# A two-layer decoder trunk: six of the seventeen chunks that TensorE transposes are turned by VectorE's block transposes and gathers from two queues

## The chip, the cores and the metric

The kernel runs on one core of one Trainium2 chip. A core has five engines that are programmed apart: TensorE (PE in the profile, with its weight loads as PEld), VectorE (DVE), ScalarE (ACT), GpSimd (POOL) and SyncE (SP). Each takes its instructions strictly in order and waits on semaphores that others raise. Data lies in the on-chip memory SBUF; TensorE writes its sums to a second memory, PSUM. DMA transfers are issued here by SP and POOL. An issue stands in the order of its engine's queue like any other instruction.

The metric is the device time of one execution in microseconds (us), lower is better. The kernel before takes 2478.81 us, the median of three runs (2478.05 to 2479.55).

## The reference

A trunk of two layers over 256 positions of width 2048, float32. Each layer is

```
h = RMSNorm(x)
q, k, v, uv, gate_logits = split(h @ w_in)                 # 2048 -> 7680
branch_a = sliding_window_attention(q, k, v) @ w_attn_branch
branch_b = chunked_sgu(gelu(uv)) @ w_sgu_branch
merged = gates_a * branch_a + gates_b * branch_b
x = x + merged @ w_out
h2 = RMSNorm(x)
x = x + (silu(h2 @ w_gate) * (h2 @ w_up)) @ w_down         # 2048 -> 5632 -> 2048
```

Nearly all of the work is products of a 256-row activation with large weights, and every weight is read once from the DRAM.

## The kernel before

**Products.** A weight is cut into column chunks of 512 (CW). A piece of 256 rows by 512 columns (a "half", 512 KB) is loaded by SP (L198, `raw`), and split into two parts whose sum keeps nearly the whole float32: ScalarE copies it to `whi` (L221), VectorE subtracts to get `wlo` (L222). The activation has to lie transposed, with the contraction along the 128 partitions, and is split the same way into `uh` and `ul`. TensorE then adds three products for each block, `uh*whi`, `uh*wlo` and `ul*whi` (L310, L311), each a matmul of 128x128 with 128x512. A half feeds 12 matmuls. Pairs of chunks (gate and up, or two columns of w_out or w_down) go by a scheme with seven products in place of eight for one quarter of the contraction. Its sums are formed by VectorE (L209 for the weights, L335 for the results), and its six first pieces, of six matmuls each, are laid between the last halves of the product before.

**Steps.** `Stream` loads seven pieces ahead (W_LOAD) and splits four ahead (W_SPLIT); there are five `raw` buffers and four of `whi` and of `wlo`. After every 12 matmuls (two of the six-matmul pieces, or one half) `tick()` runs. `after(n, fn)` puts work n ticks later, and everything beside the matmuls (norms, gelu, attention, transposes) is laid out with it. TensorE keeps the order in which the code is written; the other engines' order is made by a scheduler with a timeline of its own, so the diff alone doesn't tell where an instruction lands.

**Transposed chunks.** `transposed()` makes `uh` and `ul` of one chunk of 512 columns (a "unit"). It has two ways. With `on_pe`, TensorE transposes the chunk in eight matmuls of 128x128 against the identity (L421, tile `pt` in PSUM), and ScalarE and VectorE make `uh` and `ul` from PSUM in the same step. Without it, `turn()` lets VectorE transpose 32x32 blocks of each half of the chunk into `box` (L379, two instructions, one tick apart); 16 DMAs of 32 KB then carry the blocks to their places in `tt` (L384), issued by POOL for units of the residual and hidden chunks and by SP for queries, keys, attention outputs and the gating unit's outputs; six and seven steps after the DMAs (plus `late`), ScalarE and VectorE split `tt` into `uh` and `ul`. There is one `box` buffer.

**Which chunks go by TensorE.** Seventeen: the four of the input; the last chunk of `merged` in each layer; the last chunk of x before the feed-forward part in each layer (`nxt.unit(3)`, L859); three of the four chunks of x before the second layer; and the last hidden chunk of each of the three rounds of the feed-forward part in each layer (L949, L950). The rounds hold four, four and three chunks of 512. Each is a last chunk of an activation, produced only a few steps before the next product wants it. The product that follows a round, or follows the residual, begins with chunk 1, so the last of four chunks is wanted last.

Of the kernel before, what the change touches and what calls it, by code (L numbers as in the profile page):

```python
# [30 lines left out]
B = 32  # L31
# [26 lines left out]
def hybrid_trunk(ctx: ExitStack, tc: tile.TileContext, x, mix_norm, w_in, q_norm, k_norm, sinks,  # L58
# [313 lines left out]
    def turn(dst, src, queue):  # L372


        box = turned.tile([P, 4, 4, NT, B], F32, tag="box", name=nm("box"))
        iv = src.rearrange("p t (k j c) -> p t k j c", j=4, c=B)

        def blocks(t):
            nc.vector.transpose(box[:, :, :, t, :].rearrange("p j k r -> p k j r"), iv[:, t])  # L379

        def gather():
            for j in range(4):
                for i in range(4):
                    queue.dma_start(dst[j * B:(j + 1) * B, i], box[i * B:(i + 1) * B, j])  # L384

        blocks(0)
        after(1, lambda: (blocks(1), gather()))

    def transposed(units, c, src, cols=None, on_pe=False, wino=None, again=False, queue=None, late=0):

# [33 lines left out]
            return  # L424

        tt = slot([P, 4, 4, NT, B], name="tt")
        turn(tt, src, queue or nc.gpsimd)
# [51 lines left out]
    class Norm:  # L479
# [10 lines left out]
                nc.scalar.activation(junk, xs[:, t, c * CW:(c + 1) * CW], AF.Square,  # L490
                                     accum_out=self.ss[t][:, c:c + 1])

        def unit(self, c, on_pe=False, again=False):
            transposed(self.units, c, xs[:, :, c * CW:(c + 1) * CW], cols=self.cols[:, 4 * c:4 * c + 4],
                       on_pe=on_pe, again=again,
                       wino=None if c != WINO or on_pe else WINO_FIRST if again else WINO_IN if self.soon else
                       WINO_NORM)

# [346 lines left out]
    def residual(key, nxt=None, scale=1.0, store=False):  # L845

        def chunk(j, sums):
# [22 lines left out]
    for l in range(DEPTH):  # L870
# [65 lines left out]
        def hidden(hT, c):  # L936
# [8 lines left out]
            def on_up(up):  # L945
                for t in range(NT):
                    nc.vector.scalar_tensor_tensor(out=hid[:, t, :], in0=up[t], scalar=norm.rr[t], in1=hid[:, t, :],
                                                   op0=ALU.mult, op1=ALU.mult)
# [54 lines left out]
```

## Time and profile before

| | |
|---|---|
| median of three runs | 2478.81 us |
| profiled execution | 2476.85 us, of which the span 2475.1 us |
| TensorE (PE) busy | 2462.7 us, 99% |
| VectorE (DVE) busy | 1929.7 us, 78% |
| ScalarE (ACT) busy | 1430.2 us, 58% |
| GpSimd (POOL) busy | 282.8 us, 11% |
| DMA | 502.54 MB, 203 GB/s, queue of SP 59.8% of 16 engines |
| granted TensorE clock | 1.0 |

The span runs from the first to the last instruction of the program; the time of an execution has 1.75 us around it. A row of a timeline gives the start in us, the duration, engine, line, operation, tiles (written<-read), and in brackets how long the engine had been idle before it and what ended that. Matmuls overlap, so the distance between two starts is what one costs TensorE, not its duration. In a group's row, the numbers after the count are min/median/max in ns. A row of waits gives the engine and line that waited, whom for, us in total, times, and the longest.

### The profile page before, as it was taken

To read this page: it belongs to the slowest core of one execution; us is meant where nothing else is said; L and a number is where in the kernel's file an instruction comes from. 1 tells how busy PE (TensorE), PEld (TensorE's weight loads), DVE (VectorE), ACT (ScalarE), POOL (GpSimd) and SP (SyncE) were. 2 spreads that over 40 slices of the span, in tenths; PEclk is the share of its full clock that TensorE was granted. 3 is DMA by queue.
4 is the path that set the end of the run, shared out by engine and by line. 5 is a ranking of instruction groups with operands and counts; after the bars stand their busy time and mean duration, and the time that the engine had idled before them with its cause. 6 is when DMAs were issued, how large, how long until landed. Compare 5 with 4: busy or idle time off the path is not lost.

```text
span 2475.1 us, 31205 instructions
## 1 busy us (share of the span) xinstructions
PE 2462.7 (99%) x11088; PEld 2027.7 (82%) x11088; DVE 1929.7 (78%) x2261; ACT 1430.2 (58%) x1794; POOL 282.8 (11%) x527
## 2 busy tenths in 40 slices
PE   9999999999999999999999999999999999999999
PEld 7888888888888888888888888888888888888887
DVE  6798676887877787778887986768878777877786
ACT  5566544575655565556655665446655555655564
POOL 3100002221110111001101000121212001110110
PEclk9999999999999999999999999999999999999999
DMA  8655656576656666575747446666657566656654
GB/s 295 205 176 166 213 198 218 181 240 194 214 195 205 211 191 226 174 226 186 229 152 266 153 160 219 214 203 196 227 186 233 183 218 195 215 196 201 216 191 150
DMA packets 275661, 502.54 MB, mean 203 GB/s; under 512 B 26224, under 2 KB 36048, under 8 KB 275504
## 3 DMA queue, kind: packets, MB, share of 16 engines
q1 hardware_dynamic: 259472, 484.25, 59.8%
q0 software_dynamic: 15712, 16.01, 2.2%
q8 instruction: 87, 1.43, 0.2%
q14 instruction: 70, 0.57, 0.1%
q10 hardware_dynamic: 320, 0.27, 0.0%
HBM read 475.27 MB, written 2.10 MB: 193 GB/s over the span
## 4 chain that ended last, share of the span: by engine, by line
PE 93%; DVE 4%; issue 1%; DMA 1%; ACT 1%; SPq 0%; POOL 0%; DVEq 0%; ACTq 0%
PE acc L310 60%; PE acc L311 30%; DVE wlo L222 2%; DMA raw<-in_w_in_dram 1%; PE po L758 1%; DVE raw L209 1%; PE pt L421 1%; ACT whi L221 0%; PE psc L719 0%; PE ppt L748 0%; PE psg L836 0%; DVE ul L412 0%; DVE kept L335 0%; SPq L384 0%; DVE box L379 0%
## 5 line engine op out<-in xcount | busy, mean ns | idle before, releaser
L222 DVE TENSOR_TENSOR wlo<-raw,whi 128x1024 fp32r<-128x1024 f32 (+1 forms) x1039 | 1265.7, 1220 | 494.6 <-ACT whi L221 481.4
L221 ACT ACTIVATE whi<-raw 128x1024 fp32r<-128x1024 f32 (+1 forms) x1039 | 1098.0, 1058 | 924.6 <-PE acc L311 750.7
L310 PE MATMUL acc<-whi,uh 128*128 128x512 f32 x3114 | 1217.2, 391 | 0.4 <-ACT whi L221 0.2
L310 PE MATMUL acc<-wlo,uh 128*128 128x512 f32 x3114 | 1212.7, 389 | 1.5 <-DVE wlo L222 1.4
L311 PE MATMUL acc<-whi,ul 128*128 128x512 f32 x3114 | 1212.3, 389 | 0.0
L310 PEld LDWEIGHTS acc<-wlo,uh 128*128 128x128 f32 x3114 | 584.7, 188 | 124.5 <-DVE wlo L222 3.9
L311 PEld LDWEIGHTS acc<-whi,ul 128*128 128x128 f32 x3114 | 584.4, 188 | 122.6 <-DVE ul L412 0.2
L310 PEld LDWEIGHTS acc<-whi,uh 128*128 128x128 f32 x3114 | 584.6, 188 | 121.3 <-ACT uh L407 0.8
L384 POOL DMA_DIRECT2D tt<-box x480 | 236.0, 498 | 1714.5 <-DVE box L379 949.9
L209 DVE TENSOR_TENSOR raw<-raw,raw 128x1024 f32<-128x1024 f32 x188 | 229.3, 1220 | 1.3
L310 PE MATMUL acc<-wlo,sh 128*128 128x512 f32 x376 | 151.3, 402 | 3.3 <-DVE kept L335 3.3
L310 PE MATMUL acc<-whi,sh 128*128 128x512 f32 x376 | 147.2, 392 | 0.0
L311 PE MATMUL acc<-whi,sl 128*128 128x512 f32 x376 | 146.7, 390 | 0.0
L310 PEld LDWEIGHTS acc<-wlo,sh 128*128 128x128 f32 x376 | 70.5, 188 | 27.6 <-DVE kept L335 14.5
L311 PEld LDWEIGHTS acc<-whi,sl 128*128 128x128 f32 x376 | 70.6, 188 | 15.2
L310 PEld LDWEIGHTS acc<-whi,sh 128*128 128x128 f32 x376 | 70.7, 188 | 13.2
L335 DVE TENSOR_TENSOR kept<-acc,kept 128x512 f32<-128x512 f32 x94 | 64.1, 682 | 0.0
L338 ACT ACTIVATE acc<-kept 128x512 f32<-128x512 f32 x94 | 54.0, 587 | 8.5 <-DVE kept L335 8.3
L853 DVE SCALAR_TENSOR_TENSOR xs<-acc,xs 128x512 f32<-128x512 f32 (+1 forms) x66 | 41.2, 666 | 7.8 <-PE acc L311 7.8
L942 ACT ACTIVATE hid<-acc,rhalf 128x512 f32<-128x512 f32 x44 | 30.4, 690 | 21.0 <-PE acc L311 21.0
L332 ACT ACTIVATE kept<-acc 128x512 f32<-128x512 f32 x47 | 28.1, 597 | 15.0 <-PE acc L311 15.0
L943 DVE SCALAR_TENSOR_TENSOR hid<-hid,acc 128x512 f32<-128x512 f32 x44 | 29.6, 684 | 8.3 <-ACT hid L942 8.3
(135 smaller groups left out, 878.0 us busy)
## 6 DMA issues: line engine op xcount, KB each, us to landing
raw<-in_w_in_dram SPq DMA_DIRECT2D x239, 512.0 KB, 4.6
raw<-in_w_up_dram SPq DMA_DIRECT2D x176, 512.0 KB, 4.7
raw<-in_w_gate_dram SPq DMA_DIRECT2D x176, 512.0 KB, 4.6
raw<-in_w_down_dram SPq DMA_DIRECT2D x176, 512.0 KB, 4.6
raw<-in_w_out_dram SPq DMA_DIRECT2D x64, 512.0 KB, 4.8
raw<-in_w_attn_branch_dram SPq DMA_DIRECT2D x32, 512.0 KB, 5.5
raw<-in_w_sgu_branch_dram SPq DMA_DIRECT2D x32, 512.0 KB, 4.3
tt<-box POOLq DMA_DIRECT2D x480, 32.0 KB, 4.1
```

The lines of the kernel that those rows point to most:

```text
L209: self.last = nc.vector.tensor_tensor(out=self.raws[d], in0=self.raws[x], in1=self.raws[y], op=ALU.subtract)
L221: nc.scalar.activation(hi[:, i, :], raw[:, i, :], AF.Copy)
L222: self.last = nc.vector.tensor_tensor(out=lo[:, i, :], in0=raw[:, i, :], in1=hi[:, i, :].bitcast(F32), op=ALU.subtract)
L310: nc.tensor.matmul(ps, a, part[:, kk, :], start=first and kk + n == 0, stop=False, skip_group_check=True)
L311: nc.tensor.matmul(ps, b, hi[:, kk, :], start=False, stop=kk == 1, skip_group_check=True)
L332: nc.scalar.activation(p.kept[:, 1, :], a[0], AF.Copy)
L335: nc.vector.tensor_tensor(out=p.kept[:, int(tag == "P7"), :], in0=a[1], in1=p.kept[:, 1, :], op=ALU.add)
L338: nc.scalar.activation(ps, p.kept[:, t, :], AF.Copy)
L384: queue.dma_start(dst[j * B:(j + 1) * B, i], box[i * B:(i + 1) * B, j])
L853: nc.vector.scalar_tensor_tensor(out=xs[:, t, sl], in0=sums[t][:, i * w:(i + 1) * w], scalar=scale, in1=xs[:, t, sl], op0=ALU.mult, op1=AL ...
L942: nc.scalar.activation(th, g[t], AF.Tanh, scale=norm.rh[t])
L943: nc.vector.scalar_tensor_tensor(out=th, in0=th, scalar=1.0, in1=g[t], op0=ALU.add, op1=ALU.mult)
```

## The change

Six of the seventeen chunks go the other way: the last chunk of x before the feed-forward part (both layers) and the last hidden chunk of the two rounds with four chunks (both layers). Eleven still go by TensorE. For the six, `transposed()` is called one tick after the chunk's result in place of three, VectorE transposes the blocks, the 16 DMAs are shared by SP and POOL, eight each, and the split comes four and five steps after the start of `turn` (`late=-2`), two sooner than for other turned chunks.

```diff
         def gather():
             for j in range(4):
                 for i in range(4):
-                    queue.dma_start(dst[j * B:(j + 1) * B, i], box[i * B:(i + 1) * B, j])
+                    q = queue if queue is not None else (nc.sync, nc.gpsimd)[i % 2]
+                    q.dma_start(dst[j * B:(j + 1) * B, i], box[i * B:(i + 1) * B, j])
...
-        def unit(self, c, on_pe=False, again=False):
+        def unit(self, c, on_pe=False, again=False, queue=nc.gpsimd, late=0):
             transposed(self.units, c, xs[:, :, c * CW:(c + 1) * CW], cols=self.cols[:, 4 * c:4 * c + 4],
-                       on_pe=on_pe, again=again,
+                       on_pe=on_pe, again=again, queue=queue, late=late,
...
-                after(3 if j == NCH - 1 and not nxt.soon else 2, lambda: nxt.unit(j, j == NCH - 1 or j > 0 and nxt.soon))
+                last = j == NCH - 1 and not nxt.soon
+                after(1 if last else 2, lambda: nxt.unit(j, j > 0 and nxt.soon, queue=None if last else nc.gpsimd,
+                                                         late=-2 if last else 0))
...
-                pe = c == len(hT) - 1
-                after(3 if pe else 2, lambda: transposed(hT, c, hid, on_pe=pe, wino=WINO_HID if c == WINO else None))
+                pe, soon = c == len(hT) - 1 == 2, c == 3
+                after(3 if pe else 1 if soon else 2,
+                      lambda: transposed(hT, c, hid, on_pe=pe, wino=WINO_HID if c == WINO else None,
+                                         queue=None if soon else nc.gpsimd, late=-2 if soon else 0))
```

On TensorE the change takes out two rows of four transposes at each of the six places and moves nothing else. On the other engines the order around one hidden chunk (the first round of layer 0) and around one chunk of x (layer 0) shows what is moved. Line numbers of the changed kernel are one higher from L385 on.

VectorE at the hidden chunk, before (L947 makes the chunk, L404 splits it from `pt`):

```order
L947 TENSOR_SCALAR hid_6003<-acc_6057,rr_965_5005,hid_6003 128x512
L947 TENSOR_SCALAR hid_6003<-acc_6058,rr_969_5014,hid_6003 128x512
L222 TENSOR_TENSOR wlo_6348<-raw_6171,whi_6347 128x1024
L222 TENSOR_TENSOR wlo_6360<-raw_6312,whi_6359 128x1024
L222 TENSOR_TENSOR wlo_6398<-raw_6325,whi_6397 128x1024
L404 TENSOR_TENSOR ul_6380<-pt_6381,uh_6379 128x512
L404 TENSOR_TENSOR ul_6380<-pt_6388,uh_6379 128x512
L222 TENSOR_TENSOR wlo_6418<-raw_6345,whi_6417 128x1024
```

and after (L379 are the block transposes, L405 splits the chunk from `tt`):

```order
L379 STREAM_TRANSPOSE box_6358<-hid_6013 128x4x4x32
L222 TENSOR_TENSOR wlo_6363<-raw_6181,whi_6362 128x1024
L379 STREAM_TRANSPOSE box_6358<-hid_6013 128x4x4x32
L222 TENSOR_TENSOR wlo_6392<-raw_6322,whi_6391 128x1024
L222 TENSOR_TENSOR wlo_6414<-raw_6335,whi_6413 128x1024
L222 TENSOR_TENSOR wlo_6434<-raw_6360,whi_6433 128x1024
L222 TENSOR_TENSOR wlo_6446<-raw_6389,whi_6445 128x1024
L222 TENSOR_TENSOR wlo_6464<-raw_6411,whi_6463 128x1024
L222 TENSOR_TENSOR wlo_6484<-raw_6429,whi_6483 128x1024
L209 TENSOR_TENSOR raw_6429<-raw_6431,raw_6429 128x1024
L222 TENSOR_TENSOR wlo_6503<-raw_6443,whi_6502 128x1024
L405 TENSOR_TENSOR ul_6356<-tt_6357,uh_6355 128x512 x2
```

Two block transposes are added around the first subtraction behind the chunk, and the split moves five subtractions later. ScalarE's two copies to `uh` move the same way, behind five more `whi`.

SP at the hidden chunk, after (before, the same loads stand there without the row of `tt`):

```order
L198 DMA raw_6411<-in_w_down_dram 128x2x512
L198 DMA raw_6520<-in_w_down_dram 128x2x512
L385 DMA tt_6357<-box_6358 32x256 x8
L198 DMA raw_6443<-in_w_down_dram 128x2x512
L198 DMA raw_6481<-in_w_down_dram 128x2x512
```

Eight DMAs of the gather stand between two loads of weights; POOL has the other eight, with nothing else near them at this place.

ScalarE at the chunk of x, before (L407 scales and copies to `uh`; `tt_4727` is chunk 2, `pt` is chunk 3):

```order
L407 ACTIVATE uh_4725<-tt_4727,vcols 128x256 x4
L407 ACTIVATE uh_4952<-pt_4954,vcols 128x256 x2
L407 ACTIVATE uh_4952<-pt_4965,vcols 128x256 x2
L221 ACTIVATE whi_5020<-raw_4918 128x1024
L221 ACTIVATE whi_5032<-raw_4930 128x1024
```

and after:

```order
L408 ACTIVATE uh_4725<-tt_4727,vcols 128x256 x4
L221 ACTIVATE whi_5018<-raw_4923 128x1024
L221 ACTIVATE whi_5030<-raw_4952 128x1024
L221 ACTIVATE whi_5052<-raw_4978 128x1024
L221 ACTIVATE whi_5076<-raw_5014 128x1024
L221 ACTIVATE whi_5095<-raw_5028 128x1024
L221 ACTIVATE whi_5115<-raw_5014 128x1024
L408 ACTIVATE uh_4917<-tt_4919,vcols 128x256 x4
```

The four copies of chunk 3 move behind six weight copies. On VectorE the eight subtractions of chunk 3 (L413) move behind the same six pieces' `wlo`, and the two block transposes stand together two subtractions behind the chunk's sums (L854). On POOL the eight DMAs stand ahead of the two `rstd` of the norm. From the place of the removed transposes to the first matmul that reads the unit, TensorE's order has 102 matmuls of L310 and L311 at each of the six places.

More of the change, by code (lines that the diff above doesn't have):

```diff
@@ L383, in gather, with transposed @@
                 for i in range(4):
-                    queue.dma_start(dst[j * B:(j + 1) * B, i], box[i * B:(i + 1) * B, j])
+                    q = queue if queue is not None else (nc.sync, nc.gpsimd)[i % 2]
+                    q.dma_start(dst[j * B:(j + 1) * B, i], box[i * B:(i + 1) * B, j])
         blocks(0)
         after(1, lambda: (blocks(1), gather()))
-    def transposed(units, c, src, cols=None, on_pe=False, wino=None, again=False, queue=None, late=0):
+    def transposed(units, c, src, cols=None, on_pe=False, wino=None, again=False, queue=nc.gpsimd, late=0):
         uh, ul = units[c] if again else (slot([P, 4, S], F32R, "uh"), slot([P, 4, S], F32R, "ul"))
@@ L426, in transposed @@
         tt = slot([P, 4, 4, NT, B], name="tt")
-        turn(tt, src, queue or nc.gpsimd)
+        turn(tt, src, queue)
         def blocks_of(k0):
```

## The prediction

> **What bounds the kernel now.** I read the page first: the busy shares, the clock, the chain of work that ended last.
>
> ```profile
> span 2475.1 us, 31205 instructions
> PE 2462.7 (99%) x11088; PEld 2027.7 (82%) x11088; DVE 1929.7 (78%) x2261; ACT 1430.2 (58%) x1794; POOL 282.8 (11%) x527
> PEclk9999999999999999999999999999999999999999
> PE 93%; DVE 4%; issue 1%; DMA 1%; ACT 1%; SPq 0%; POOL 0%; DVEq 0%; ACTq 0%
> ```
>
> TensorE is the bound in every slice, at full clock, and 93% of the chain is its matmuls. Whatever leaves its queue shortens the program, unless it then waits. So the next view is its waits, taken from 45 us on to leave out the start (the last row, ScalarE's, is of the whole span):
>
> ```profile
> PEld acc L310 <- DVE kept L335: 15.0, 42, 1.3
> PEld acc L310 <- DVE wlo L222: 0.4, 1, 0.4
> PE acc L310 <- DVE kept L335: 3.3, 4, 0.9
> ...
> ACT uh L403 <- DMA tt<-box: 9.3, 5, 3.4
> ```
>
> In 2430 us TensorE waited once, for 0.4 us, for a split weight. The rows of `kept` belong to the sums of the seven-product scheme, which the change leaves alone. Loads, splits and the turns that SP carries already are hidden.
>
> **What a transposed chunk costs TensorE.** The timeline of TensorE at a hidden chunk and at a chunk of x:
>
> ```profile
> 720.41 0.40 PE L311 MATMUL acc<-whi,ul 128*128 128x512 f32 x1
> 720.64 1.04 PE L421 MATMUL pt<-ident,hid 128*128 128x128 f32 x8
> 721.44 0.48 PE L310 MATMUL acc<-whi,uh 128*128 128x512 f32 x1
> ...
> 550.45 0.39 PE L311 MATMUL acc<-whi,ul 128*128 128x512 f32 x1
> 550.68 1.04 PE L421 MATMUL pt<-ident,xs 128*128 128x128 f32 x8
> 551.47 0.48 PE L310 MATMUL acc<-whi,uh 128*128 128x512 f32 x1
> 551.78 0.40 PE L310 MATMUL acc<-wlo,uh 128*128 128x512 f32 x1
> ...
> 2205.99 1.03 PE L421 MATMUL pt<-ident,hid 128*128 128x128 f32 x8
> 2206.78 0.48 PE L310 MATMUL acc<-whi,uh 128*128 128x512 f32 x1
> ...
> L421 PE MATMUL pt<-ident,hid x48: 270/272/273, 720.6 to 2421.9; 128*128 128x128 f32 x48
> ```
>
> Matmuls start 0.23 us apart (550.45 to 550.68). Eight transposes hold the next matmul back from 720.64 to 721.44, 0.80 us, and the one after it comes 0.31 us later (551.47 to 551.78) in place of 0.23, another 0.08. No wait stands in these rows. One chunk therefore costs 0.88 us, and the last of the six places reads the same (2205.99 to 2206.78). Six chunks: 6 x 0.88 = 5.3 us, all of it on the engine that sets the end.
>
> The Trainium skill ("TensorE: Matmul & The Clock Gate", Part 4: PE-mode transpose) gives about 275 ns for one such transpose in a kernel's context; by that as a price, 48 of them would be worth an estimated 13.2 us. The rows agree with it as a duration (272 ns) and not as a price, since eight of them take 0.80 us.
>
> **What is added, engine by engine.**
>
> ```profile
> L379 DVE STREAM_TRANSPOSE box<-hid x32: 700/705/708, 593.6 to 2376.2; 128x512 f32<-128x512 f32 x32
> L404 DVE TENSOR_TENSOR ul<-tt,uh x44: 647/684/692, 210.4 to 2396.8; 128x512 fp32r<-128x512 f32 x44
> L404 DVE TENSOR_TENSOR ul<-pt,uh x16: 677/681/684, 466.3 to 2424.2; 128x512 fp32r<-128x512 f32 x16
> ...
> 716.56 1.40 DVE L947 SCALAR_TENSOR_TENSOR hid<-acc,rr,hid 128x512 f32<-128x512 f32 x2
> 717.90 2.58 DVE L222 TENSOR_TENSOR wlo<-raw,whi 128x1024 fp32r<-128x1024 f32 x2
> 721.98 1.23 DVE L222 TENSOR_TENSOR wlo<-raw,whi 128x1024 fp32r<-128x1024 f32 x1 [1.50 <-ACT whi L221]
> ```
>
> VectorE gets two block transposes for each chunk, 2 x 0.705 = 1.41 us. The split costs the same from `tt` as from `pt` (684 and 681 ns). At the hidden chunk the two stand before 721.98, where VectorE was idle for 1.50 us, so they fit and cost nothing. At the chunk of x the eight subtractions of chunk 3 (2.16 us in the rows below) leave the crowded stretch as the 1.41 us enter it, so VectorE is earlier there.
>
> ```profile
> 550.11 1.23 DVE L222 TENSOR_TENSOR wlo<-raw,whi 128x1024 fp32r<-128x1024 f32 x1 [0.95 <-ACT whi L221]
> 555.50 2.16 DVE L412 SCALAR_TENSOR_TENSOR ul<-pt,vcols,uh 128x128 fp32r<-128x128 f32 x8
> 567.87 1.23 DVE L222 TENSOR_TENSOR wlo<-raw,whi 128x1024 fp32r<-128x1024 f32 x1 [1.54 <-ACT whi L221]
> 570.59 2.59 DVE L222 TENSOR_TENSOR wlo<-raw,whi 128x1024 fp32r<-128x1024 f32 x2 [1.49 <-ACT whi L221]
> ...
> 551.89 1.69 ACT L407 ACTIVATE uh<-tt,vcols 128x256 fp32r<-128x256 f32 x4
> 566.77 1.06 ACT L221 ACTIVATE whi<-raw 128x1024 fp32r<-128x1024 f32 x1 [1.71 <-PE acc L311]
> ...
> 734.01 1.06 ACT L221 ACTIVATE whi<-raw 128x1024 fp32r<-128x1024 f32 x1 [1.66 <-PE acc L311]
> ```
>
> **Is the unit there in time?** By the order, 102 matmuls lie between the removed transposes and the first reader. At 0.23 us each that is 23.5 us: 744.1 at the hidden chunk, 574.2 at the chunk of x. At the hidden chunk ScalarE's copies stand behind the `whi` of 734.01, so from 735.1 on, and `ul` follows by about 737.6: over 6 us to spare. At the chunk of x the copies stand behind the `whi` of 566.77, from 567.8 on; VectorE's eight subtractions follow the `wlo` of 567.87, from 569.1 for 2.2 us, to 571.3: 2.9 us to spare. These starts are set by TensorE's own progress ("<-PE acc L311"), so all move earlier together.
>
> The copies must also find `tt` landed.
>
> ```profile
> L384 POOL DMA_DIRECT2D tt<-box x480: 496/498/570, 45.5 to 2386.8; - x160
> L384 SPq DMA_DIRECT2D tt<-box x192: 507/588/1082, 88.0 to 1550.3; - x192
> DMA to landing us min/median/max: 1.6/3.8/8.4
> ...
> 1540.87 10.01 SPq L384 DMA_DIRECT2D tt<-box  x16
> 1550.98 2.06 SPq L198 DMA_DIRECT2D raw<-in_w_attn_branch_dram  x4
> ...
> 719.15 1.73 SPq L198 DMA_DIRECT2D raw<-in_w_down_dram  x2
> raw<-in_w_down_dram SPq DMA_DIRECT2D x176, 512.0 KB, 4.6
> ```
>
> `box` is full at about 717.9 + 0.7 + 1.2 + 0.7 = 720.5 at the hidden chunk and, behind the `wlo` that ends at 551.3, at 552.7 at the chunk of x. POOL issues eight in 8 x 0.5 = 4 us. With the longest landing seen, 8.4 us, `tt` is there by 732.9 and 565.1, each over 2 us ahead of the copies. POOL's two `rstd` at the chunk of x come some 2 us later; `hid` needs them only at the first gate, far behind.
>
> On SP the eight issues stand ahead of a load. The nearest row is a turn of sixteen: 10.01 us, no load in between, then the loads catch up. Twelve such turns (192 issues) are in the trace, and the row of waits above bounds what they cost TensorE at 0.4 us in all. Half a turn, 5 us, is bounded by 0 below and by 0.4/12 = 0.03 us for each above; I take 0. Above that lies only a wait that adds up with another, which the rivals price. A gain beyond 5.3 has no source I can see: none of the six places had TensorE waiting.
>
> **The sum.** -5.3 us on TensorE, 0 from VectorE, ScalarE, SP and POOL. From the profiled execution, 2476.85 - 5.3 = 2471.5. That execution lies 1.96 us below the median of the runs, 2478.81, and the forecast is made for the median: 2473.5 us, -0.21%. A difference of 0.2%, 5.0 us, is about what a measurement of this kernel can tell from no change, so the forecast lies just beyond that bound.
>
> **Rivals.**
>
> *Given back in part.* One or two of the places return what they save, as a wait for `ul` or for a sum of the seven-product scheme that VectorE's displaced work delays. For it: the two places at x have only 2.9 us of slack, and behind them VectorE works without a break from 570.59 to 573.2. Against: VectorE's idle time of 1.5 us ahead of most `wlo`. Two places lost: -3.5 us, 2475.3.
>
> *POOL's DMAs starve (slower).* If each of POOL's eight issues had to wait for a subtraction of `wlo` (1.23 us, row 567.87), they would take 8 x 1.7 = 13.8 us; with 8.4 us to land, `tt` is there at 552.7 + 22.2 = 574.9 at x and 742.7 at the hidden chunk. ScalarE would stand at the copies for 7 us. `ul` would come at about 578.5 at x (a copy, a `wlo` and 2.2 us later) against 574.2, and at 745.3 at the hidden chunk (two copies and two splits) against 744.1: 2 x 4.3 + 4 x 1.2 = 13.4 us, net +8.1, 2486.9. It turns to a loss when the eight issues take over 12 us, since from 9.5 us on each more costs the two places at x as much: 2 x (12.2 - 9.5) = 5.4. The rows speak against it: 480 issues between 496 and 570 ns while VectorE is 78% busy. The Trainium skill ("SBUF — State Buffer", SBUF: two separate sides) describes just this, POOL unable to write descriptors while VectorE holds a shared port in a two-port mode; no row here shows it.
>
> *SP blocks the weights (slower).* Behind the eight gathers the load that was issued at about 720.5 (the second in the row of 719.15) comes 5 us later. It is first read by the `whi` of 734.01, and loads land in 4.6 us, so its slack is 734.0 - 720.9 - 4.6 = 8.5 us. That `whi` starts when TensorE is done with the fourth piece ahead, so three pieces of 12 x 0.23 us lie between, 8.3, less 1.06 and 1.23 for the split: 6 more. SP could stand for 14.5 us; each us beyond costs TensorE one at each place, and from 15.4 on (5.3 / 6 = 0.9) the change loses. At 16.5 it would be 6 x 2 - 5.3 = +6.7, 2485.5. The row of 10.01 us speaks against it.
>
> *Transposes dearer than their spacing.* 48 x 0.273 = 13.1 us gained, 2465.7, if they did not overlap; the rows show that they do.
>
> **How the numbers follow.** Forecast 0.74, given back in part 0.12, POOL 0.05, SP 0.07, dearer transposes 0.02. Within the forecast, the spread of the runs (2478.05 to 2479.55) puts about five sixths beyond the bound, 0.61, and 0.13 within it. So faster 0.61 + 0.02 = 0.63, the same 0.13 + 0.12 = 0.25, slower 0.12. The range reaches from 2471.5, the forecast less the 2 us by which an execution may lie below the median, over the places given back to 2478.0, where four of six chunks' saving and more is lost; the two slower cases and the last lie outside, 0.14.
>
> **What would show it.** TensorE's instructions fall by 48 and its busy time by about 5 us; the rows of `pt` keep 88 transposes; the wait of L310 for `wlo` stays under 1 us and none for `ul` at the six places appears; `box` rows rise by 12, of about 0.705 us; SP's `tt` rises to 240, POOL's to 528. The prediction is wrong if TensorE waits for `ul` some 23 us behind the removed transposes, or for `wlo` behind SP's gathers, or if ScalarE's waits for "DMA tt<-box" grow far over the 9.3 us that they have now.

## The result, and the profile after

The changed kernel takes 2473.74 us, the median of eleven runs (2472.88 to 2476.05), against 2479.82 us for the kernel before in as many runs taken beside them (2478.05 to 2481.61). The ratio is 0.9977, 95% interval 0.9969 to 0.9985: faster by 0.23%, just past the 0.2% that the prediction takes for what tells a change from none, with an interval that reaches to both sides of that bound. A later measurement (below) gives 0.9976 [0.9967, 0.9985].

The page of the changed kernel, the same rows as of before. Its profiled execution takes 2473.22 us:

```profile
span 2471.5 us, 31351 instructions
PE 2457.8 (99%) x11040; PEld 2024.3 (82%) x11040; DVE 1935.8 (78%) x2273; ACT 1431.4 (58%) x1794; POOL 305.6 (12%) x575
PE 90%; DVE 4%; DMA 2%; issue 1%; SPq 1%; ACT 1%; POOL 0%; DVEq 0%; ACTq 0%
```

TensorE has 48 instructions less and is busy 4.9 us less. VectorE has 12 block transposes more, POOL and SP 48 gathers more each. The waits from 45 us on, of the same kinds as before:

```profile
PEld acc L310 <- DVE kept L335: 15.0, 42, 1.3
...
ACT uh L404 <- DMA tt<-box: 8.1, 6, 3.1
...
PE acc L310 <- DVE kept L335: 3.3, 4, 0.9
...
PEld acc L310 <- DVE wlo L222: 1.0, 2, 0.7
```

No wait for `ul` is there. The two waits for `wlo` lie before 400 us, ahead of the first of the six places at 551 us.

How one chunk goes now, read from the timelines of five engines: the first hidden chunk, and then the first chunk of x.

```profile
718.11 0.70 DVE L379 STREAM_TRANSPOSE box<-hid 128x512 f32<-128x512 f32 x1
...
719.84 0.70 DVE L379 STREAM_TRANSPOSE box<-hid 128x512 f32<-128x512 f32 x1
...
722.22 1.23 DVE L222 TENSOR_TENSOR wlo<-raw,whi 128x1024 fp32r<-128x1024 f32 x1 [0.57 <-ACT whi L221]
...
735.56 1.29 DVE L405 TENSOR_TENSOR ul<-tt,uh 128x512 fp32r<-128x512 f32 x2
...
720.66 6.26 SPq L385 DMA_DIRECT2D tt<-box  x8
721.08 3.90 POOL L385 DMA_DIRECT2D tt<-box  x8 [30.32 <-DVE box L379]
...
734.28 1.13 ACT L404 ACTIVATE uh<-tt 128x512 fp32r<-128x512 f32 x2
...
720.65 0.39 PE L311 MATMUL acc<-whi,ul 128*128 128x512 f32 x1
720.88 0.39 PE L310 MATMUL acc<-whi,uh 128*128 128x512 f32 x1
...
744.00 0.39 PE L310 MATMUL acc<-whi,uh 128*128 128x512 f32 x1
```

TensorE passes 720.65 without a break, where 0.80 us stood before. `box` is full at 720.5, SP issues its eight until 726.9, POOL until 725.0; the last lands at 728.8. ScalarE's copies come only at 734.3, because of their place in its order, `ul` is done at 736.9, and the first matmul that reads the unit starts at 744.0: 7.2 us to spare. The other three hidden chunks have 7.2 us as well.

```profile
552.36 1.30 DVE L379 STREAM_TRANSPOSE box<-xs 128x512 f32<-128x512 f32 x2
553.72 5.12 SPq L385 DMA_DIRECT2D tt<-box  x8
554.29 2.45 POOL L385 DMA_DIRECT2D tt<-box  x5 [12.00 <-ACT uh L408]
559.40 1.47 POOL L385 DMA_DIRECT2D tt<-box  x3 [2.66 <-issue]
567.95 1.70 ACT L408 ACTIVATE uh<-tt,vcols 128x256 fp32r<-128x256 f32 x4
569.22 2.19 DVE L413 SCALAR_TENSOR_TENSOR ul<-tt,vcols,uh 128x128 fp32r<-128x128 f32 x8
574.90 0.39 PE L310 MATMUL acc<-whi,uh 128*128 128x512 f32 x1
```

Here `ul` is done at 571.4, 3.5 us ahead of the reader at 574.9, at both chunks of x. The closest thing is the landing: POOL pauses for 2.66 us after five issues, its last gather lands at 566.1, and the copies start at 567.95.

The time between the same matmul of L310 and L311 in the two traces shows where the gain sits (worked out from the starts of all 10470 of them): it falls by 0.89 to 0.93 us at each of the six places, at 551, 721, 976, 1782, 1952 and 2207 us, 5.4 us in all, and no more than 0.1 us comes back behind any of them. The rest of the medians' difference of 6.1 us is spread between executions: the steps elsewhere, in the start-up and at 1356 us, differ from run to run. In this pair of executions the changed one is 1.1 us behind when it reaches the first place, so the spans differ by only 3.6 us.

### The profile page after: what moved, and what is told of

Its sections match the earlier page's. It is cut to its first block, busy times and chain, and to the rows that moved or that the text cites. A ratio compares the mean times of both kernels' runs of the same rounds, so it can differ in the third digit from the quotient of the medians.

```text
span 2471.5 us, 31351 instructions
## 1 busy us (share of the span) xinstructions
PE 2457.8 (99%) x11040; PEld 2024.3 (82%) x11040; DVE 1935.8 (78%) x2273; ACT 1431.4 (58%) x1794; POOL 305.6 (12%) x575
## 4 chain that ended last, share of the span: by engine, by line
PE 90%; DVE 4%; DMA 2%; issue 1%; SPq 1%; ACT 1%; POOL 0%; DVEq 0%; ACTq 0%
PE acc L310 59%; PE acc L311 29%; DMA raw<-in_w_in_dram 2%; DVE wlo L222 2%; SPq L385 1%; PE po L759 1%; ACT whi L221 1%; DVE raw L209 1%; PE ppt L749 0%; PE psc L720 0%; PE pt L422 0%; DVE box L379 0%; PE psg L837 0%; POOL rq L282 0%; DVE ul L413 0%
## 5 line engine op out<-in xcount | busy, mean ns | idle before, releaser
L310 PE MATMUL acc<-whi,uh 128*128 128x512 f32 x3114 | 1217.8, 391 | 0.8 <-ACT uh L408 0.8
L310 PE MATMUL acc<-wlo,uh 128*128 128x512 f32 x3114 | 1214.0, 390 | 2.2 <-DVE wlo L222 2.2
L311 PE MATMUL acc<-whi,ul 128*128 128x512 f32 x3114 | 1213.5, 390 | 0.0
L310 PEld LDWEIGHTS acc<-wlo,uh 128*128 128x128 f32 x3114 | 585.2, 188 | 124.8 <-DVE wlo L222 4.6
L311 PEld LDWEIGHTS acc<-whi,ul 128*128 128x128 f32 x3114 | 584.9, 188 | 122.1 <-DVE ul L413 0.2
L310 PEld LDWEIGHTS acc<-whi,uh 128*128 128x128 f32 x3114 | 585.0, 188 | 121.7 <-ACT uh L408 1.6
L385 POOL DMA_DIRECT2D tt<-box x528 | 258.6, 497 | 1713.2 <-DVE box L379 641.4
L310 PE MATMUL acc<-wlo,sh 128*128 128x512 f32 x376 | 151.6, 403 | 3.3 <-DVE kept L335 3.3
L310 PE MATMUL acc<-whi,sh 128*128 128x512 f32 x376 | 147.5, 392 | 0.0
L311 PE MATMUL acc<-whi,sl 128*128 128x512 f32 x376 | 146.9, 391 | 0.0
L310 PEld LDWEIGHTS acc<-wlo,sh 128*128 128x128 f32 x376 | 70.6, 188 | 27.7 <-DVE kept L335 14.6
L311 PEld LDWEIGHTS acc<-whi,sl 128*128 128x128 f32 x376 | 70.6, 188 | 15.2
L310 PEld LDWEIGHTS acc<-whi,sh 128*128 128x128 f32 x376 | 70.7, 188 | 13.2
L335 DVE TENSOR_TENSOR kept<-acc,kept 128x512 f32<-128x512 f32 x94 | 64.1, 682 | 0.0
L854 DVE SCALAR_TENSOR_TENSOR xs<-acc,xs 128x512 f32<-128x512 f32 (+1 forms) x66 | 41.2, 666 | 7.8 <-PE acc L311 7.8
```

The source lines that it names most:

```text
L310: nc.tensor.matmul(ps, a, part[:, kk, :], start=first and kk + n == 0, stop=False, skip_group_check=True)
L311: nc.tensor.matmul(ps, b, hi[:, kk, :], start=False, stop=kk == 1, skip_group_check=True)
L335: nc.vector.tensor_tensor(out=p.kept[:, int(tag == "P7"), :], in0=a[1], in1=p.kept[:, 1, :], op=ALU.add)
L385: q.dma_start(dst[j * B:(j + 1) * B, i], box[i * B:(i + 1) * B, j])
L854: nc.vector.scalar_tensor_tensor(out=xs[:, t, sl], in0=sums[t][:, i * w:(i + 1) * w], scalar=scale, in1=xs[:, t, sl], op0=ALU.mult, op1=AL ...
```

## The experiments

Each kernel differs from the changed one by the edit shown. "Before" is always the kernel before, run on the same chip.

### Are 48 transposes on TensorE the whole gain?

After each of the six chunks TensorE also transposes the chunk as it did before, into a PSUM tile that nothing reads; the unit still comes by the gathers.

```diff
+    def dead(src):
+        for b in range(2):
+            pt = ps_tr.tile([P, 2, S], F32, tag="tr", name=nm("pd"))
+            for kk in range(2):
+                k = 2 * b + kk
+                for t in range(NT):
+                    nc.tensor.transpose(pt[:, kk, t * P:(t + 1) * P], src[:, t, k * P:(k + 1) * P], ident)
...
+                if last:
+                    after(3, lambda: dead(xs[:, :, j * CW:(j + 1) * CW]))
...
+                if soon:
+                    after(3, lambda: dead(hid))
```

> The changed kernel with the six chunks turned by VectorE as in the change, and beside that the 48 transposes back on TensorE, three steps behind the chunk, into a PSUM tile that nobody reads. Theory (the gain is TensorE's 48 transposes and nothing else): 6 x 0.88 = 5.3 us come back, the time is that of the kernel before, within 1 us, and the start of each later matmul moves by about 0.88 at each of the six places and nowhere else. Rival (the gain came from relief of PSUM, of ScalarE or of VectorE around the places): the time stays within 1 us of the changed kernel, 6 us under the kernel before.

Measured: 2479.79 us, before 2479.22; ratio 1.0002 [0.9993, 1.0011]. The whole gain is gone. The timeline of TensorE at the first hidden chunk (`pd` is the unread tile):

```profile
720.80 0.40 PE L311 MATMUL acc<-whi,ul 128*128 128x512 f32 x1
721.04 1.03 PE L396 MATMUL pd<-ident,hid 128*128 128x128 f32 x8
721.83 0.48 PE L310 MATMUL acc<-whi,uh 128*128 128x512 f32 x1
722.14 0.40 PE L310 MATMUL acc<-wlo,uh 128*128 128x512 f32 x1
```

From 721.04 to 721.83 is 0.79 us, and the next start is 0.31 behind, as it was before the change. Against the changed kernel the matmuls move back by 0.89 to 0.93 us at each of the six places, 5.4 us in all. The 12 box transposes, the 96 gathers and the later split are in this kernel too, and it is level with before: together they cost nothing that can be measured.

### What do the sooner steps and the second queue bring?

Three kernels take the change's three handles apart. The first turns the six chunks as all others are turned, with the usual steps and POOL alone:

```diff
-                after(1 if last else 2, lambda: nxt.unit(j, j > 0 and nxt.soon, queue=None if last else nc.gpsimd,
-                                                         late=-2 if last else 0))
+                after(2, lambda: nxt.unit(j, j > 0 and nxt.soon, queue=nc.gpsimd))
...
-                after(3 if pe else 1 if soon else 2,
+                after(3 if pe else 2,
                       lambda: transposed(hT, c, hid, on_pe=pe, wino=WINO_HID if c == WINO else None,
-                                         queue=None if soon else nc.gpsimd, late=-2 if soon else 0))
+                                         queue=nc.gpsimd))
```

> The six chunks are turned in the way all other turned chunks of x and of the hidden layer are: two steps behind the chunk in place of one, the split six and seven steps on in place of four and five, all 16 gathers on POOL. The built order has ScalarE's copies two weight pieces later than in the changed kernel at all six places. Theory of the slack (7.2 us at the four hidden chunks, 3.5 us at the two chunks of x, read from the changed kernel's trace; between those pieces lie some 2.7 + 1.4 us): the hidden chunks stay in time, the chunks of x come 0 to 1.5 us late, so 0 to 3 us are lost of the gain: 3 to 6 us under the kernel before. Rival (the sooner steps and the second queue are needed, as three steps of 2.7 us each are 8.2 us, against slacks of 7.2 and 3.5): 4 x 1.0 + 2 x 4.7 = 13.4 us lost, 7 us above the kernel before.

Measured: 2475.35 us, before 2479.22; ratio 0.9983 [0.9974, 0.9993]. Most of the gain is there without either. The loss expected at the two chunks of x does not show in its trace; what is lost there is lost at the hidden chunks (below). Then the sooner start with POOL alone:

```diff
-                after(1 if last else 2, lambda: nxt.unit(j, j > 0 and nxt.soon, queue=None if last else nc.gpsimd,
+                after(1 if last else 2, lambda: nxt.unit(j, j > 0 and nxt.soon, queue=nc.gpsimd,
...
-                                         queue=None if soon else nc.gpsimd, late=-2 if soon else 0))
+                                         queue=nc.gpsimd, late=-2 if soon else 0))
```

> The changed kernel with all 16 gathers of the six chunks on POOL; the turn starts as soon as in the changed kernel, so that the start alone is kept and the second queue taken away. Theory: the second queue does what the sooner steps are said to do, since POOL alone needs 8 to 11 us for the gathers and lands later; by the built order the copies stand two pieces of weight later than in the changed kernel, as they did in the kernel with the usual steps. So the trace reads as there: 0.27 us more at each of the four hidden chunks, about 1.1 us, 2475 with before at 2479. Rival: the sooner start is what counts, and nothing shows at the hidden chunks, 2473.7.

And the usual start with both queues:

```diff
-                after(1 if last else 2, lambda: nxt.unit(j, j > 0 and nxt.soon, queue=None if last else nc.gpsimd,
+                after(2, lambda: nxt.unit(j, j > 0 and nxt.soon, queue=None if last else nc.gpsimd,
...
-                after(3 if pe else 1 if soon else 2,
+                after(3 if pe else 2,
```

> The changed kernel with the six turns started after two ticks in place of one, as other turned chunks are; both queues are kept. Theory: nothing, since the copies stand at the same piece of weight in the built order and the gathers of 5 to 7 us land well before them: 2473.7, no wait for the unit, and the six places read 0.8 to 0.9 us each as in the changed kernel. Rival: the start one tick (2.7 us) later takes the 2.9 us of slack at the two chunks of x, and TensorE waits there for the unit, 1 to 2 us in all, 2475.5.

Measured, on one chip with before at 2478.59: POOL alone 2475.20 us, ratio 0.9985 [0.9976, 0.9995]; the usual start 2473.40 us, ratio 0.9978 [0.9968, 0.9988]. The two intervals overlap, so the verdict rests on the traces. With both queues and the usual start TensorE's matmuls show no step at the six places against the changed kernel, and the slacks are the same 7.2 and 3.5 us. With POOL alone they show +0.27, +0.27, +0.25 and +0.26 us some 30 us behind the four hidden chunks, 1.1 us, and the kernel with the usual steps shows the same four. They are waits for sums of the seven-product scheme. The wait of the weight loads, POOL's gathers and ScalarE's copies of the kernel with POOL alone:

```profile
PEld acc L310 <- DVE kept L335: 16.0, 42, 1.3
...
721.13 4.40 POOL L385 DMA_DIRECT2D tt<-box  x9 [30.15 <-DVE box L379]
726.17 0.50 POOL L385 DMA_DIRECT2D tt<-box  x1 [0.63 <-DMA tt<-box]
727.96 1.47 POOL L385 DMA_DIRECT2D tt<-box  x3 [1.30 <-DMA tt<-box]
730.07 1.47 POOL L385 DMA_DIRECT2D tt<-box  x3 [0.63 <-DMA tt<-box]
...
739.82 1.14 ACT L404 ACTIVATE uh<-tt 128x512 fp32r<-128x512 f32 x2
```

The 42 waits for `kept` grow from 15.0 to 16.0 us. Sixteen gathers on POOL take 10.4 us, not 16 x 0.5 = 8: from the tenth on POOL waits for a landing. The built program says why. POOL's DMAs take eight completion semaphores in turn (`DMASW0` to `DMASW7`), and a DMA first waits for the one eight before it:

```
26 L385 DMA tt_87_524<-box_88_525 32x256 [waits DMASW2_49,DVE_49]
27 L385 DMA tt_87_524<-box_88_525 32x256 [waits DMASW3_49]
...
34 L385 DMA tt_87_524<-box_88_525 32x256 [waits DMASW2_49]
```

So POOL has at most eight gathers on the way. Eight on POOL pass at 0.49 us each, and the other eight on SP find a set of semaphores of their own. With POOL alone the last gather lands at 735.6, and the scheduler puts ScalarE's copies two pieces of weight later (739.8 in place of 734.3). VectorE's `ul` then enters at 741.1 a stretch in which VectorE is idle for 0.7 us in all until the sum that TensorE waits for, and that sum (L335) starts at 754.47 in place of 754.14.

The steps named in the change do less than they say. The built order with `late=0` in place of -2 is row for row that of the changed kernel on every engine (seen in the order only, not run): the number of steps is the earliest place, and the scheduler puts the copies later anyway. A start one tick sooner moves, at the four hidden chunks, the box transposes one `wlo` forward and SP's gathers one load forward, and nothing at the chunks of x.

### All sixteen gathers on SP

```diff
-                after(1 if last else 2, lambda: nxt.unit(j, j > 0 and nxt.soon, queue=None if last else nc.gpsimd,
+                after(1 if last else 2, lambda: nxt.unit(j, j > 0 and nxt.soon, queue=nc.sync if last else nc.gpsimd,
...
-                                         queue=None if soon else nc.gpsimd, late=-2 if soon else 0))
+                                         queue=nc.sync if soon else nc.gpsimd, late=-2 if soon else 0))
```

> As the changed kernel, with all 16 gathers of the six chunks on SP, so that the loads of weights stand for about 10 us behind them and not 5. Theory (a load has 8.5 us to spare until ScalarE reads it, and TensorE another 6 behind that, 14.5 together): TensorE sees nothing, the time is that of the changed kernel within 1 us; ScalarE waits for loads some 1 to 2 us at each place. Rival (SP's queue is the next bound): the extra 5 us are lost in part at each place, 6 x 2 = 12 us or more above the changed kernel.

Measured: 2472.38 us, before 2479.22; ratio 0.9969 [0.9958, 0.9980]. SP's queue at the first hidden chunk:

```profile
721.85 11.30 SPq L385 DMA_DIRECT2D tt<-box  x16
733.26 11.09 SPq L198 DMA_DIRECT2D raw<-in_w_down_dram  x8
```

SP loads no weight for 11.4 us and TensorE waits nowhere behind it. The copies come one piece sooner (slacks of 6.3 us at x and 7.8 to 8.6 at the hidden chunks). At the first hidden chunk the last gather lands at 734.4 and the copies start 0.3 us later. That landing is 12.7 us behind the full `box`, against 15.0 with POOL alone and 8.3 with both queues, so what sets POOL alone apart is more the scheduler's place for the copies than the landing. Whether it is better than the split was asked again with both on one chip, below.

### How long can SP stand?

Beside SP's eight gathers of each of the six chunks stand 24 small DMAs of 4 KB into a tile that nothing reads (the scheduler puts a few of them ahead of the gathers, the rest behind):

```diff
+    scr = const.tile([P, CW // 2], F32, name="scr")
...
+            if queue is None:
+                for n in range(24):
+                    i, m = n % 4, n // 4
+                    nc.sync.dma_start(scr[i * B:(i + 1) * B, m * B:(m + 1) * B], box[i * B:(i + 1) * B, i, 0, 0, :])
```

> The changed kernel with 24 more DMAs of 4 KB each on SP behind each of the six gathers, from the box into a tile that nothing reads; the computation is whole. At 0.59 us an issue SP stands for 32 x 0.59 = 18.8 us before the next load of weights (it stood 5 to 6 us in the changed kernel). Theory (the prediction's working): up to 14.5 us is hidden, each us beyond costs TensorE one at each place, so 4.3 us x 6 = 26 us more than the changed kernel, about 2500, as waits for whi or wlo some 10 to 20 us behind the gathers. Rival A, there is no slack in the loads and the changed kernel was saved by something else: 6 x 13 = 78 us more, about 2552. Rival B, the slack is larger than 14.5 us by a third or more: no wait, 2474.

Measured: 2521.99 us, before 2479.18; ratio 1.017 [1.0156, 1.0183], 48 us over the changed kernel, between the theory's 26 and rival A's 78. The queue of SP, ScalarE and TensorE behind the first hidden chunk, and two stretches with the granted clock (the number after POOL's):

```profile
724.25 1.78 SPq L390 DMA_DIRECT2D scr<-box  x3
726.40 6.08 SPq L386 DMA_DIRECT2D tt<-box  x8
732.52 13.25 SPq L390 DMA_DIRECT2D scr<-box  x21
745.88 18.33 SPq L199 DMA_DIRECT2D raw<-in_w_down_dram  x10
...
750.28 3.01 ACT L222 ACTIVATE whi<-raw 128x1024 fp32r<-128x1024 f32 x3 [13.20 <-DMA raw<-in_w_down_dram]
...
751.39 0.79 PE L311 MATMUL acc<-whi,uh 128*128 128x512 f32 x1 [5.89 <-ACT whi L222]
752.65 0.79 PE L311 MATMUL acc<-wlo,uh 128*128 128x512 f32 x1 [0.47 <-DVE wlo L223]
753.24 0.63 PE L312 MATMUL acc<-whi,ul 128*128 128x512 f32 x1
753.67 0.63 PE L311 MATMUL acc<-whi,uh 128*128 128x512 f32 x1
...
745.40:751.30 5.90, 0.10 (x1) 0.00 (x0) 0.00 (x0) 1.02 (x2) 0.00 (x0) 0.89 0.66 195
751.40:756.60 5.20, 4.73 (x10) 3.41 (x11) 5.20 (x5) 2.95 (x3) 0.00 (x0) 0.50 1.04 389
```

Here SP stood from 724.25 to 745.88, 21.6 us, more than the 18.8 I had put, because the small DMAs and the loads wait for semaphores too. By the prediction's 14.5 us TensorE should lose 21.6 - 14.5 = 7.1. The two gaps in its matmuls are 6.27 (745.11 to 751.39) and 1.26 us, less 0.23 each: 7.1. At the first chunk of x SP stood 20.3 us, 5.8 by the rule, and the gaps come to 4.6. At all four hidden chunks the gaps are within 0.3 us of the rule, at the chunks of x 1.2 and 1.3 us below it, so the threshold of 14.5 us, which was worked out for a hidden chunk, holds there.

The rest is the clock. After the gap the granted clock is 0.50, and matmuls start 0.43 us apart in place of 0.23 for some 4 us. Over the six places the matmuls fall behind by 50.3 us in this trace, of which the gaps are 37.0; the other 13.3, 2.2 us at each place, is TensorE running at half speed. The Trainium skill ("TensorE: Matmul & The Clock Gate", Part 1: The HAM clock gate) states that the clock falls to half after an idle window of about 3.4 us and comes back after as long a busy one. The trace agrees: gaps of 3.8 to 6.5 us, and seven to eleven slow matmuls behind each. Shorter waits came with the half clock too: two of 2.1 and 2.5 us in the kernel with chunk 1 (below), and one of 1.9 us in the kernel with POOL alone (last section).

### Can more chunks be turned?

Two of the eleven that stay on TensorE are last hidden chunks of the short rounds, where the next product wants them sooner. They are turned from both queues at the earliest step that the copies can take:

```diff
                 pe, soon = c == len(hT) - 1 == 2, c == 3
-                after(3 if pe else 1 if soon else 2,
+                pe, soon = False, c == len(hT) - 1
+                after(1 if soon else 2,
...
-                                         queue=None if soon else nc.gpsimd, late=-2 if soon else 0))
+                                         queue=None if soon else nc.gpsimd, late=(-4 if len(hT) == 3 else -2) if soon else 0))
```

> Eight chunks: also the last hidden chunk of the rounds with three chunks is turned by VectorE (both layers), with the split two steps sooner still, since the next product reads it 42 matmuls behind the old transposes and not 102. Theory (a turn takes some 20 us from the chunk to its split, of which 12 are the landing of the gathers, and here only 4.1 + 42 x 0.227 = 13.6 us are there): TensorE waits 2 to 6 us for the unit at each of the two places, less 0.88 for the transposes: 2 to 10 us above the changed kernel. Rival (the turn can be squeezed in): two more times 0.88, 1.8 us under the changed kernel.

Measured: 2471.56 us, before 2479.22; ratio 0.9968 [0.9955, 0.9980]. My theory fell: nothing like 2 to 10 us is lost. Against the changed kernel the matmuls gain 0.89 us at 1190 and 0.90 at 2418; the first is kept, the second is lost again (0.88 us) by 2439, part of it in waits for the unit. In layer 0 the turn takes 16 us: box from 1183.1 to 1187.0, gathers issued until 1194.3 and landed at 1196.4, copies at 1196.6, `ul` done at 1199.0, while the reader starts at 1198.1. It can start before `ul` is done because each unit is split in two halves and the first matmuls read only the first half. What I had wrong was to require the whole unit at the first matmul.

A seventh chunk of this kind beside the six from SP alone (the short round of layer 0; layer 1 left to TensorE):

```diff
-                pe, soon = c == len(hT) - 1 == 2, c == 3
+                soon = c == len(hT) - 1 and (c == 3 or l == 0)
+                pe = c == 2 and len(hT) == 3 and not soon
...
+                                         queue=(nc.sync if c == 3 else None) if soon else nc.gpsimd,
+                                         late=(-2 if c == 3 else -4) if soon else 0))
```

> Seven chunks turned: the six with all 16 gathers on SP, which was as good as the split, and the last hidden chunk of the short round of layer 0, split over both queues and at the earliest step; that of layer 1, which gave its 0.9 us back at the end, stays with TensorE. Theory: the savings add up, 7 x 0.88 = 6.2 us under the kernel before, 2472.6 to 2473 by a median of 2479 for before, 0.9 less than the changed kernel. Rival: the longer stand of SP (10 us) at the place ahead of the short round takes some of it, 2474 or more.

Measured: 2473.31 us, before 2479.18; ratio 0.9972 [0.9962, 0.9983], no better than six. Against the six from SP the matmuls gain 0.89 us at 1191 and lose 1.26 by 1218. The two waits in TensorE's timeline:

```profile
1200.34 0.50 PE L310 MATMUL acc<-whi,uh 128*128 128x512 f32 x1 [0.34 <-ACT uh L404]
...
1216.03 0.50 PE L310 MATMUL acc<-wlo,uh 128*128 128x512 f32 x1 [0.16 <-DVE kept L335]
```

The gathers were issued until 1197.5 and landed 10.7 us after the box was full, against 9.4 in the kernel with eight, and that is enough to make the reader wait. SP's last gather waits in both for a load of weights ahead of it, which takes 8.9 us from issue to landing here and 7.4 in the kernel with eight; why isn't shown. Neither side had it: SP's stand of 10 us is far from this place, but the saving did not add up either.

Then chunk 1 of x before the second layer:

```diff
-                after(1 if last else 2, lambda: nxt.unit(j, j > 0 and nxt.soon, queue=None if last else nc.gpsimd,
-                                                         late=-2 if last else 0))
+                early = last or j < 2 and nxt.soon
+                after(1 if early else 2, lambda: nxt.unit(j, j > 1 and nxt.soon, queue=None if early else nc.gpsimd,
+                                                          late=-2 if last or j == 1 and nxt.soon else 0))
```

> The changed kernel with a seventh chunk turned: chunk 1 of x before the second layer, the middle one of the three that TensorE keeps there; chunk 0, turned already, is started a tick sooner and gathered from both queues, so that the one box is free. The eight transposes of chunk 1 stood there at a place that shows 1.67 us, 0.88 of transposes and 0.79 of a wait. Theory: by the built order ScalarE's copies of the chunk stand next to the piece whose matmuls read it first (zero pieces ahead, against 2 at the six places), so the first reader waits, 1 to 4 us for one chunk: 2473 to 2477, same or slower than the changed kernel by up to 3 us. Rival: as with the short rounds, where the copies stand one piece behind the first reader's and one of the two places still gave its 0.9 us, the first half of the unit suffices: -0.9 to -1.7 us against the changed kernel, 2472.

Measured: 2477.64 us, before 2479.18; ratio 0.9993 [0.9983, 1.0002], 4 us over the changed kernel: the theory's direction, a larger price, and another wait than the one expected. TensorE behind the place, what the two waits were for, and the stretch after the second:

```profile
1243.06 0.50 PE L310 MATMUL acc<-whi,uh 128*128 128x512 f32 x1 [2.09 <-ACT uh L453]
1243.40 0.40 PE L310 MATMUL acc<-wlo,uh 128*128 128x512 f32 x1
1246.32 0.79 PE L311 MATMUL acc<-whi,ul 128*128 128x512 f32 x1 [2.53 <-DVE ul L454]
1246.91 0.63 PE L310 MATMUL acc<-whi,uh 128*128 128x512 f32 x1
...
1241.97 1.04 ACT L453 ACTIVATE uh<-flat 128x1024 fp32r<-128x1024 f32 x1
...
1245.05 1.22 DVE L454 TENSOR_TENSOR ul<-flat,uh 128x1024 fp32r<-128x1024 f32 x1
...
1246.30:1251.00 4.70, 4.68 (x12) 3.61 (x13) 3.47 (x12) 0.00 (x0) 0.00 (x0) 0.50 0.35 107
```

The transposes' place gives 1.8 us, two waits of 2.1 and 2.5 us take 4.6, and the half clock behind them takes most of the rest of the 8.0 us by which the matmuls fall behind from 1217 to 1251. L453 and L454 split chunk 0 of the same x, which was turned before the change too. In this kernel chunk 1's copies (1.7 us on ScalarE from 1239.3) and subtractions (2.2 us on VectorE from 1241.8) stand just ahead of them, and no matmul waits for chunk 1 itself. So chunk 1's work makes chunk 0 late; how much of it is due to the sooner start of chunk 0, which this run changes as well, isn't separated.

### Side by side on one chip

The changed kernel, the one with all sixteen gathers on SP and the one with eight chunks, on one chip in five rounds each:

> The changed kernel itself, on the same chip as the two that follow, since a difference of 1 to 2 us between kernels measured on different chips settles nothing. Expected: 5 to 6 us under the kernel before.

> The six chunks with all 16 gathers on SP, beside the changed kernel. Theory: both hide the turn in full at all six places, so they are equal within 1 us. Rival: the copies that stand one piece earlier save something that the trace does not show, and it is 1 to 1.5 us under the changed kernel as the earlier runs on different chips had it.

> The eight chunks, with the last hidden chunk of the short rounds turned too, beside the changed kernel. Theory (by the trace of the earlier run): 0.9 us kept at layer 0 and nothing at layer 1, so 0.9 us under the changed kernel. Rival: the turn of the short round is at the edge in layer 0 too, as in the kernel with seven, and it is equal to the changed kernel or up to 0.9 us slower.

Measured, with before at 2479.06: 2473.11 us, 0.9976 [0.9967, 0.9985]; 2473.01 us, 0.9975 [0.9965, 0.9985]; 2472.40 us, 0.9975 [0.9962, 0.9987]. All sixteen on SP is equal to the split, as expected: outside the start-up its matmuls differ by 0.3 us, and the 1.4 us of the earlier runs was spread. For eight chunks the trace again keeps 0.89 us at 1190 us and gains 0.89 at 2417, of which it gives back 0.3; 0.7 us in the medians is less than the spread, and whether it beats the changed kernel stays open.

## Why the prediction was right

Forecast 2473.5 us, measured 2473.74 and 2473.11. That the times agree within 0.4 us is partly luck: the forecast took 5.3 us from a median of three runs, 2478.81, the eleven runs have 2479.82, and the medians fell by 6.1 and 5.9 us. The traces, free of that spread, give 5.4. By its steps:

**The price of a chunk on TensorE** (0.80 + 0.08 = 0.88 us) is right: 0.89 to 0.93 at the six places, 5.4 us in all against 5.3, and putting the transposes back costs the same 5.4. The rival of the dearer transposes (13.1 us by their duration) is refuted by this, and with it a price made of the figure that the prediction takes from the Trainium skill ("TensorE: Matmul & The Clock Gate", Part 4: PE-mode transpose). The page gives some 275 ns for bf16; these transposes, in float32, last 272 ns, but eight of them take 0.8 us on TensorE's path, since they overlap.

**Nothing from the other engines** is right: the kernel with the transposes put back carries all added work and is level with before. At the hidden chunk the forecast of the times holds within 1 us: box full 720.5 (measured 720.5), POOL done 724.5 (725.0), copies 735.1 (734.3), `ul` 737.6 (736.9), reader 744.1 (744.0), slack "over 6" (7.2). At the chunk of x box 552.7 (553.7), copies 567.8 (568.0), `ul` 571.3 (571.4), reader 574.2 (574.9), slack 2.9 (3.5). The copies' time came out so well because it was read from the order and not from the number of steps.

**The landing of `tt`** was forecast at 732.9 at the latest for the hidden chunk and came at 728.8; but at the chunk of x the pause of POOL brought it to 566.1, where I had put 565.1 at the latest. 1.8 us were left, so it cost nothing.

**SP blocks the weights.** The term of zero for half a turn holds, and so does the threshold: 11.4 us cost nothing, and at the hidden chunks some 21 us cost what lies beyond 14.5. What the rival's price left out is the half clock behind each wait, 2.2 us a place in the run with the long stand; its 16.5 us stand would have cost more than the 2 us that I gave it if its wait is long enough to drop the clock, which was not tried.

**POOL's DMAs starve.** Not seen. POOL's eight go in 3.9 us at five of the six places, with a subtraction of VectorE in the middle (722.22). Sixteen take longer, for the semaphores' sake. The one pause at the sixth place has another cause (below).

**Given back in part.** No place gave anything back, but the mechanism that I named, VectorE's displaced work in front of a sum of the scheme, is what the kernels with POOL alone show: 0.27 us at the four hidden chunks. I had looked for it at the two chunks of x, where `ul` then came 1.9 us after the reader had started and TensorE did not wait, since the first half was there.

**How near it is to no change.** The forecast was -0.21%, just past its own bound of 0.2%, and the measured -0.23% lies as near to it.

## What to carry to other kernels

When one engine bounds every slice, price what leaves its queue by the distance between starts and not by durations, and then look for the next reader of what was moved, in the built order rather than in the numbers that ask for it; here a turn needs some 16 us from the chunk to the split unit, a place with 26 us between chunk and reader hides it whole, and one with 15 us does not do so reliably. A burst of sixteen small transfers stalls on POOL, where at most eight are on the way and one took 3.5 to 5.6 us to land at the first hidden chunk; a second queue helped there, but SP alone, whose last gathers landed 1.8 us after their issue, did as well. Gathers may stand in front of loads for as long as the loads' slack lasts. Past that slack each wait of TensorE of 4 to 6 us cost its length and some 2 us more for the clock.

## What the hardware showed that was not expected

**A short wait of TensorE costs more in some executions than in others.** At 1353 to 1357 us (1361 in the kernel with chunk 1 and 1378 in the one with the long stand), in each of the fourteen traces, TensorE waits 1.5 to 2.0 us for a transposed table of layer 1. The matmul that ends the wait and the stretch behind it, in the changed kernel:

```profile
1354.56 0.66 PE L749 MATMUL ppt<-ident,pr 128*128 128x128 f32 x4 [1.82 <-DVE wsT L620]
...
1356.00:1358.00 2.00, 2.00 (x10) 1.68 (x9) 2.00 (x3) 0.89 (x2) 0.00 (x0) 1.00 0.62 235
```

and in the kernel with POOL alone:

```profile
1355.18 0.66 PE L749 MATMUL ppt<-ident,pr 128*128 128x128 f32 x4 [1.92 <-DVE wsT L620]
...
1356.00:1358.00 2.00, 2.00 (x7) 1.56 (x6) 2.00 (x4) 1.51 (x3) 0.00 (x0) 0.56 0.94 340
```

The first keeps the full clock, the second falls to 0.56 and loses 1.7 us there; the kernel with the transposes put back, the one with the usual start and the one with the long stand fall too, and the other ten traces don't. The length of the wait alone doesn't decide: 1.92 us here and 1.79 with the usual start come with the fall, 1.92 with the usual steps and 1.82 in the changed kernel without. The wait stands between small matmuls (eight transposes and eight of 64 rows ahead of it, four transposes behind), and no run separates what they add. Part of the spread of the runs is of this kind: of 76 runs of the kernel before, 25 with a mean granted clock of 1.0 have a median of 2478.0 us, and 15 with 0.998 have 2480.6. That the moment of the wait decides is my reading; no run here sets it.

**POOL pauses after a fixed number of DMAs.** The pause of 2.66 us at the first chunk of x is not VectorE's doing. Counted over the trace, POOL stops for 2.6 to 2.7 us after its 128th DMA in each of the fourteen traces, at 600 us in the kernel before and at 557 in the changed one, whatever work stands there, and for 2.7 to 2.9 us after its 249th. In the changed kernel the 128th happens to fall into the turn with the least time before its copies. What the pause is isn't shown.
